# Second product of two feed-forward blocks by a seven-product scheme in two of its three parts, with a weight difference in PSUM and a bias table in another block

## The chip, the core and the metric

The kernel runs on one core of one Trainium2 chip. The metric is device time in microseconds (us), the median of three runs. The engines are called as in the profile: PE (TensorE matmul), PEld (its weight load), DVE (VectorE), ACT (ScalarE), POOL (GpSimd) and SP, which issues most of the DMAs. All data are float32. A matmul whose accuracy matters is made of three: both factors are cut into a high part H (rounded to the type `fp32r`) and a low part L (the rest), and the kernel adds up WH·XH, WH·XL and WL·XH.

## The reference

One step of a two-layer decoder on 512 prompt tokens and 64 sample tokens, which the kernel treats as one matrix of T = 576 columns. The change concerns the feed-forward blocks, of which there are two in each layer (four in all), with D_MODEL = 1024 and D_FF = 2816:

```
def swiglu(x, wi, wo):
    gate, up = jnp.split(x @ wi, 2, axis=-1)
    return (jax.nn.silu(gate) * up) @ wo

for i in range(DEPTH):                     # DEPTH = 2
    h = h + 0.5 * swiglu(rms_norm(h, w['norm_w'][i, 0]), w['ffn1_wi'][i], w['ffn1_wo'][i])
    h = h + mixer(rms_norm(h, w['norm_w'][i, 1]))      # layer 0: RWKV-7; layer 1: windowed attention
    h = h + 0.5 * swiglu(rms_norm(h, w['norm_w'][i, 2]), w['ffn2_wi'][i], w['ffn2_wo'][i])
    h = h + jax.nn.sigmoid(rms_norm(h, w['norm_w'][i, 3]) @ w['pe_gate'][i]) * (p[i] @ w['pe_proj'][i])
```

The attention of layer 1 adds to its logits a bias that depends on the distance alone: three tables, made once from `rel_bias` by a product with a one-hot matrix.

## The kernel before

Everything lies transposed: features on the 128 partitions, the 576 tokens on the free axis, in two halves of HF = 288 columns. So h is eight tiles of 128x576, and the hidden vector of a block has FT = 22 tiles. `ffn` (L368) runs one block. For each hidden tile j a **unit** makes the gate tile, the up tile and u = silu(gate)·up. Units 0 to 4 are plain (`pair`, L375). From unit F_STD = 5 on a unit is `pair7` (L396): gate and up tile, the two halves of the eight k-tiles and the two column halves make a 2x2 by 2x2 block product, which a Strassen-Winograd scheme does in seven block products instead of eight. Each is 4 k-tiles x 3 = 12 matmuls of 128x288, so a unit has 84.

The seven left factors are sums of weight blocks, made in `seven` (L324) for each unit: four loads of 128x512 (`wr`, `sr`), then three sums s1, s2, s4 on DVE into PSUM (L348), one difference s3 = w11 - w21 on POOL into SBUF (L359, tile `ss`), and seven splits (`form`, L337): ACT copies H (L340), and L = a - H (L343) comes from DVE for the three sums in PSUM and from POOL for the other four. The right factors are made once for each block (`forms`, L286). The sums of a unit in PSUM go out through ACT copies to `ev` (L410) and DVE additions (L416, L452); POOL makes the second half of u (L453), and u is split (L159 on ACT, L160 on POOL) into `hv`.

The second product, hidden times `wo`, is plain. It is done in parts, `F_PARTS = (0, 7, 14, FT)`: when the units of a part and one more are through, `wo_part` (L457) takes for each of the eight output tiles n the part's 7 or 8 k-tiles, 3 matmuls each, for both halves; weights are loaded and split by `load_w` (L163: ACT L174, POOL L175), and DVE adds each half to h (L463). The last part has no unit behind it to run ahead. While it runs, `feed` (L217) prepares the next stage as each h tile is done: squares on ACT, their sum on DVE (L273, tile `ssum`), and, where the next stage wants them, the scaled tile's H on ACT (L266) and L on DVE (L267).

`run` calls the blocks in phases with SBUF and PSUM pools of their own: f0 (first block of layer 0), r (RWKV), f1 (second block of layer 0, the gated input `ple`, K and V, first block of layer 1), at (attention) and f2 (second block of layer 1, `ple`). The bias tables are made in f0, by three insertions behind units 9, 12 and 16 (`bias_table`, L1326). In f0 the last part also loads and splits four tiles for `ple` (`ple_load`, L486).

A scheduler sets the order on each engine from the dependencies and the buffers. So weights of a unit are formed while the unit before it runs; `after` (L153) holds some steps behind others. PSUM has eight banks: here four `ps_e`, two `ps_q` and two `ps_d` (`pg`).

Of the kernel before, what the change touches and what calls it, by code (L numbers as in the profile page):

```python
# [16 lines left out]
D = 1024  # L17
DT = D // 128
# [35 lines left out]
N_S7 = 4  # L54
F_PARTS = (0, 7, 14, FT)
# [34 lines left out]
class Body:  # L90
# [124 lines left out]


    def feed(self, *gains, spill=False, start=False, early=(1, S_AT)):  # L217
# [15 lines left out]
        def f(k, half=None):  # L233

            h = self.h[k]
            if half is not None:
                sl = slice(half * HF, (half + 1) * HF)
                sq = self.s(*sv[1]) if k else ssum
# [24 lines left out]
            sq = self.s(*sv[1]) if k else ssum  # L263
# [22 lines left out]
    def forms(self, gain):  # L286
# [7 lines left out]
        def sums(k):  # L294
# [3 lines left out]
            c, e, d = self.bank("q", HF), self.bank("q", HF), self.s("u", 2)[:, h0]  # L298
# [25 lines left out]
    def seven(self, w0, w1, prev):  # L324

        nc = self.nc
        n = DT // 2 * 128
        raw, out = {}, {}
        for i, (nm, w, k) in enumerate((("11", w0, 0), ("21", w1, 0), ("22", w1, n), ("12", w0, n))):
# [4 lines left out]
            nc.sync.dma_start(r, w[:, k:k + n])  # L334
            raw[nm] = r

        def form(i, a, eng):  # L337
# [3 lines left out]
            if not i and prev:  # L341
                self.after(c, prev[1])
            eng.tensor_tensor(L, a, H.bitcast(F32), op=ALU.subtract)  # L343
            out[i] = [(H[:, k * 128:(k + 1) * 128], L[:, k * 128:(k + 1) * 128]) for k in range(DT // 2)]
# [13 lines left out]
        s3 = self.ph.tile([128, n], F32, name="ss", tag="ss", bufs=1)  # L358
        i = nc.gpsimd.tensor_tensor(s3, raw["11"], raw["21"], op=ALU.subtract).ins  # L359
        if prev and prev[2]:  # L360
            self.after(i, prev[2])
        form(4, s3, nc.gpsimd)
# [5 lines left out]
    def ffn(self, wi, wo, done, pre=None, mid=None, fast=None, side=None):  # L368
# [4 lines left out]
        self.n_hv, self.n_t1 = N_HF, 4  # L373

        def pair(j):  # L375
            t1 = self.s("t1", self.n_t1)
            u = self.s("u", 2)
# [15 lines left out]
            hist[j] = self.last_u, hist[j][0], None  # L393
            hv[j] = self.split(u, self.s("hv", self.n_hv, F32R), self.s("hv", self.n_hv, F32R))

        def pair7(j, X):  # L396
            h0, h1 = slice(0, HF), slice(HF, T)
            W = self.seven(wi[j], wi[FT + j], hist[j - 2])
            t1, u = self.s("t1", self.n_t1), self.s("u", 2)
# [54 lines left out]
            hv[j] = self.split(u, self.s("hv", self.n_hv, F32R), self.s("hv", self.n_hv, F32R), nc.gpsimd)  # L454
            hist[j] = i, silu, self.last_l
# [14 lines left out]
        ends = F_PARTS if fast else (0, FH, FT)  # L470
        steps, X = self.forms(fast) if fast else ((), None)
        j = 0
        for a, b in zip(ends, ends[1:]):
# [10 lines left out]
            wo_part(list(range(a, b)), b == FT)  # L484

    def ple_load(self):  # L486
        nc = self.nc
        px = []
        for i in range(2):
            for k in range(PD // 128):  # L490
                p = self.s("u", 2)
# [16 lines left out]
    def ple(self, i, done, tail=False):  # L508
# [760 lines left out]
    def shared_kv(self):  # L1269
# [17 lines left out]
        for n, t in enumerate(ts):  # L1287
# [38 lines left out]
    def bias_table(self, g):  # L1326
# [12 lines left out]
        tr = self.sm("tr", [16, SKW])  # L1339
        nc.vector.tensor_copy(tr, tb[:, TBW - 1 - SKW:TBW - 1][:, ::-1])  # L1340
        nc.scalar.dma_start(self.rev[g * 16:(g + 1) * 16], tr)
# [358 lines left out]
    def run(self):  # L1700
        nc, I = self.nc, self.I
        self.st_tag = (("ssum", 1), ("sq", 2))
        with self.phase("f0", d="e", e=4, q=2, st="q"):
# [11 lines left out]
            self.bias_load()  # L1715
            self.ffn(I["f1wi"][0], I["f1wo"][0], lambda: self.feed(spill=True), pre, self.bias_table, fast="n00", side=self.ple_load)
# [138 lines left out]
```

## Time and profile before

| | us |
|---|---|
| three runs | 2852.56, 2854.98 (median), 2858.19 |
| the profiled execution | 2856.38 |
| its span, first to last instruction | 2854.6 |
| PE busy | 2723.1 (95%) |
| PEld busy | 2540.6 (89%) |
| DVE busy | 1556.9 (55%) |
| POOL busy | 1518.1 (53%) |
| ACT busy | 1298.3 (45%) |

PE is the busy one; the others are busy half of the time on average, which says little of a single stage. So the stages are read one by one: f0's block lies at about 60 to 427 us, the two blocks of f1 at 1110 to 1490 and 1600 to 1990, and that of f2 at 2390 to 2787.

### The profile page before, as it was taken

How to read it: one execution, taken by the hardware profiler on the slowest of the kernel's cores; microseconds unless marked ns; L12 is line 12 of the kernel's file. 1: busy time of each engine (PE TensorE's matmuls, PEld its weight loads, DVE VectorE, ACT ScalarE, POOL GpSimd, SP SyncE). 2: the span in 40 equal slices, each digit the busy share in tenths (PEclk: the TensorE clock that was granted, in tenths of full speed). 3: DMA queues.
4: the chain of work that ended last, by engine and by line, in shares of the span. 5: the costliest groups of instructions: out<-in, count | busy, mean ns of one | idle time of the engine just before them, and what ended most of it. 6: DMA issues, size and time to landing. Idle time of an engine off the chain costs nothing. (4 is left out here: it accounts for less than half of the span.)

```text
span 2854.6 us, 56186 instructions
## 1 busy us (share of the span) xinstructions
PE 2723.1 (95%) x21952; PEld 2540.6 (89%) x21952; DVE 1556.9 (55%) x3300; ACT 1298.3 (45%) x2568; POOL 1518.1 (53%) x1254
## 2 busy tenths in 40 slices
PE   8999997988999999999999999999899999999997
PEld 8999997976767778999999999999888879999997
DVE  6543538457577756633436554243577776533435
ACT  4443535444333225434445444354556655443544
POOL 5665747544243335756654466674544325766753
PEclk9999998999999999999999999999999999999999
DMA  4232234222112112232333223324434443222222
GB/s 137 79 96 85 85 113 139 71 62 55 53 44 75 40 45 80 84 91 85 96 98 103 95 80 95 89 82 120 113 86 104 132 150 115 79 92 86 93 86 96
DMA packets 177085, 257.80 MB, mean 90 GB/s; under 512 B 46889, under 2 KB 70897, under 8 KB 176820
## 3 DMA queue, kind: packets, MB, share of 16 engines
q1 hardware_dynamic: 149312, 224.74, 25.9%
q10 hardware_dynamic: 27508, 29.48, 3.9%
q8 instruction: 172, 2.82, 0.4%
q14 instruction: 93, 0.76, 0.1%
HBM read 234.31 MB, written 19.85 MB: 89 GB/s over the span
## 5 line engine op out<-in xcount | busy, mean ns | idle before, releaser
L175 POOL TENSOR_TENSOR wl<-wr,wh 128x512 fp32r<-128x512 f32 (+2 forms) x477 | 603.3, 1274 | 722.4 <-ACT wh L174 679.9
L201 PE MATMUL ps_e<-hv,wh 128*128 128x288 f32 x2944 | 587.3, 295 | 2.5 <-POOL hv L160 1.3
L174 ACT CAST wh<-wr 128x512 fp32r<-128x512 f32 (+2 forms) x477 | 277.4, 587 | 539.2 <-PE ps_e L201 293.2
L201 PEld LDWEIGHTS ps_e<-hv,wh 128*128 128x128 f32 x2944 | 472.2, 188 | 3.9 <-POOL hv L160 2.2
L201 PE MATMUL ps_e<-hv,wl 128*128 128x288 f32 x1472 | 434.1, 295 | 1.2 <-POOL wl L175 1.2
L558 PE MATMUL ps_d<-x,wh 128*128 128x288 f32 x1664 | 367.6, 308 | 9.1 <-ACT wh L174 3.2
L201 PE MATMUL ps_e<-x,wh 128*128 128x288 f32 x1792 | 364.8, 299 | 11.2 <-ACT x L266 6.9
L201 PEld LDWEIGHTS ps_e<-x,wh 128*128 128x128 f32 x1792 | 291.6, 190 | 13.1 <-ACT x L266 6.9
L558 PEld LDWEIGHTS ps_d<-x,wh 128*128 128x128 f32 x1664 | 273.5, 191 | 29.7 <-issue 9.3
L201 PEld LDWEIGHTS ps_e<-hv,wl 128*128 128x128 f32 x1472 | 276.3, 188 | 1.5 <-POOL wl L175 1.4
L463 DVE SCALAR_TENSOR_TENSOR h<-ps_e,h 128x288 f32<-128x288 f32 x192 | 87.6, 457 | 328.0 <-PE ps_e L201 327.9
L201 PE MATMUL ps_e<-x,wl 128*128 128x288 f32 x896 | 265.6, 297 | 0.0
L558 PE MATMUL ps_d<-x,wl 128*128 128x288 f32 x832 | 249.9, 301 | 0.3 <-POOL wl L175 0.3
L406 PE MATMUL ps_e<-x,wh 128*128 128x288 f32 x1056 | 214.4, 296 | 0.0
L343 POOL TENSOR_TENSOR wl<-wr,wh 128x512 fp32r<-128x512 f32 x136 | 197.0, 1452 | 18.6 <-ACT wh L340 12.7
L406 PEld LDWEIGHTS ps_e<-x,wh 128*128 128x128 f32 x1056 | 170.3, 189 | 3.9 <-issue 3.9
L406 PE MATMUL ps_e<-TH,wh 128*128 128x288 f32 x544 | 162.1, 298 | 9.7 <-DVE t L380 6.9
L201 PEld LDWEIGHTS ps_e<-x,wl 128*128 128x128 f32 x896 | 169.9, 190 | 0.1
L558 PEld LDWEIGHTS ps_d<-x,wl 128*128 128x128 f32 x832 | 158.7, 191 | 2.2 <-issue 0.5
L406 PE MATMUL ps_e<-TH,wl 128*128 128x288 f32 x544 | 160.4, 295 | 0.0
L406 PE MATMUL ps_e<-TL,wh 128*128 128x288 f32 x544 | 159.9, 294 | 0.0
L406 PE MATMUL ps_e<-x,wl 128*128 128x288 f32 x528 | 155.7, 296 | 0.0
(413 smaller groups left out, 6390.3 us busy)
## 6 DMA issues: line engine op xcount, KB each, us to landing
wr<-in_f1wi SPq DMA_DIRECT2D x108, 256.0 KB
wr<-in_f2wi SPq DMA_DIRECT2D x108, 256.0 KB
sr<-in_f1wi SPq DMA_DIRECT2D x68, 256.0 KB
sr<-in_f2wi SPq DMA_DIRECT2D x68, 256.0 KB
wr<-in_f1wo SPq DMA_DIRECT2D x64, 256.0 KB
wr<-in_f2wo SPq DMA_DIRECT2D x64, 256.0 KB
wr<-in_wrkv SPq DMA_DIRECT2D x48, 256.0 KB
wr<-in_wq SPq DMA_DIRECT2D x48, 256.0 KB
```

Source lines behind the costliest of these rows:

```text
L174: nc.scalar.copy(H, raw)
L175: nc.gpsimd.tensor_tensor(L, raw, H.bitcast(F32), op=ALU.subtract)
L201: nc.tensor.matmul(ps[0:nw], a, b[:, sl], start=k + m == 0, stop=3 * k + m == n - 1)
L343: eng.tensor_tensor(L, a, H.bitcast(F32), op=ALU.subtract)
L406: nc.tensor.matmul(ps, a, b, start=first and k + m == 0, stop=k == DT // 2 - 1 and m == 2, skip_group_check=True)
L463: nc.vector.scalar_tensor_tensor(h[:, sl], ps, 0.5, h[:, sl], op0=ALU.mult, op1=ALU.add)
L558: self.nc.tensor.matmul(out, lhsT, rhs, **kw)
```

## The change

In the blocks of f0 and f2 (`deep`) the parts become (0, 6, 14, 22). The first stays plain; the second and the third, 8 hidden tiles each, do the product with `wo` by the same seven-product scheme: two output tiles by two hidden tiles by two column halves, 4 pairs of hidden tiles in a part (`wo_part7`). The left factors come from `seven`, now called with four blocks of `wo`, each a load of four separate runs of 128 columns per partition. The right factors are made from the u tiles of two units (`pair_forms`). All `seven` calls, in all four blocks, make s3 on DVE into a `ps_d` bank and its L on DVE. The tables of the bias move from f0 to the first block of f1, their reversed copy in two halves. `ssum` and `sq` share the buffers of other tiles, and there are three `u` buffers instead of two.

```diff
+N_U = 3
+N_EV = 5
+N_HD = 28
+D_PARTS = (0, 6, 14, FT)
@@ seven
-        s3 = self.ph.tile([128, n], F32, name="ss", tag="ss", bufs=1)
-        i = nc.gpsimd.tensor_tensor(s3, raw["11"], raw["21"], op=ALU.subtract).ins
-        form(4, s3, nc.gpsimd)
+        s3 = self.pg.tile([128, 512], F32, name="ps_d", tag="d")[:, 0:n]
+        nc.vector.tensor_tensor(s3, raw["11"], raw["21"], op=ALU.subtract)
+        form(4, s3, nc.vector)
@@
+    def pair_forms(self, a, b, quick):
+        c, d = self.s("t1", self.n_t1), self.ph.tile([128, HF], F32, name="ev", tag="ev", bufs=N_EV)
+        nc.vector.tensor_tensor(c[:, h0], a[:, h1], a[:, h0], op=sub)
+        nc.vector.tensor_tensor(c[:, h1], b[:, h1], a[:, h1], op=sub)
+        nc.vector.tensor_tensor(d, b[:, h1], c[:, h0], op=sub)
+        nc.vector.tensor_tensor(a[:, h1], b[:, h0], d, op=sub)
+        for i, x in enumerate((c, a, b)):
+            out.append(self.split(x, ..., nc.vector if quick and i < 2 else nc.gpsimd))
+        self.split(d, D[:, 0], D[:, 1], nc.gpsimd)
@@ pair7
-            hv[j] = self.split(u, ..., nc.gpsimd)
+            if j < first7:
+                hv[j] = self.split(u, ..., nc.gpsimd)
+            elif (j - first7) % 2 == 0:
+                pairs[j] = u
+            else:
+                pairs[j - 1] = self.pair_forms(pairs[j - 1], u, j == FT - 1)
@@
+        def wo_part7(js, last):
+            X = [pairs[j] for j in js[0::2]]
+            for n in range(0, DT, 2):
+                W = self.seven(...)
+                if last and not n:
+                    steps = ((C, 1, 0), (A, 0, 4), (B, 3, 5))
+                    for ps, i, x in steps:
+                        prod(ps, i, x, True, range(len(X) - 1))
+                    for ps, i, x in steps:
+                        prod(ps, i, x, False, (len(X) - 1,))
+                    to_h(C, 1, h1)
+                    to_h(A, 0, h0)
+                    to_h(B, 0, h0)
+                    prod(C, 5, 6, False)
+                    to_h(C, 0, h1)
+                    prod(A, 2, 2, False)
+                    to_h(A, 0, h1)
+                    prod(A, 4, 1, False)
+                    to_h(A, 1, h1)
+                else:
...
+                prod(A, 6, 3, False)
+                to_h(A, 1, h0)
+                if f:
+                    f(n)
+                    f(n + 1)
@@ bias_table
-        tr = self.sm("tr", [16, SKW])
+        for c in (0, SKW // 2):
+            tr = self.sm("tr", [16, SKW // 2])
@@ run
-            self.bias_load()
-            self.ffn(I["f1wi"][0], ..., self.bias_table, fast="n00", side=self.ple_load)
+            self.ffn(I["f1wi"][0], ..., fast="n00", side=self.ple_load, deep=True)
+                self.bias_load()
+                self.ffn(I["f2wi"][0], ..., self.pre, self.bias_table, fast="n02")
-            self.ffn(I["f2wi"][1], ..., self.pre, fast="n12")
+            self.ffn(I["f2wi"][1], ..., self.pre, fast="n12", deep=True)
```

`to_h` is the old addition to h (DVE, L525 of the changed kernel, L463 of the old one), seven of them for two output tiles, each behind one of the seven products.

The order moves on DVE in two places. The first is a pair of seven-product units, unit 11 of f0's block before and unit 21 after (`t`, `u` and `ev` are the unit's own tiles, L448 is the old L416; `ps_q`, `sl`, `wl` are weight sums and low parts for the next unit). Before:

```order
L348 TENSOR_TENSOR ps_q<-sr,wr 128x512
L343 TENSOR_TENSOR sl<-ps_q,sh 128x512
L348 TENSOR_TENSOR ps_q<-ps_q,wr 128x512
L343 TENSOR_TENSOR wl<-ps_q,wh 128x512
L348 TENSOR_TENSOR ps_q<-sr,ps_q 128x512
L416 TENSOR_TENSOR t_2365<-ps_d,ev 128x288
L343 TENSOR_TENSOR sl<-ps_q,sh 128x512
L416 TENSOR_TENSOR ev<-ps_e,ev 128x288
L416 TENSOR_TENSOR t_2365<-ps_e,ev 128x288
L452 TENSOR_TENSOR u<-ps_e,t_2365 128x288
```

After, from s3 (L369) on:

```order
L369 TENSOR_TENSOR ps_d<-wr,sr 128x512
L353 TENSOR_TENSOR wl<-ps_q,wh 128x512
L358 TENSOR_TENSOR ps_q<-sr,ps_q 128x512
L448 TENSOR_TENSOR t_4433<-ps_d,ev 128x288
L382 TENSOR_TENSOR t_4535<-u 128x288
L353 TENSOR_TENSOR sl<-ps_q,sh 128x512
L448 TENSOR_TENSOR ev<-ps_e,ev 128x288
L353 TENSOR_TENSOR wl<-ps_d,wh 128x512
L448 TENSOR_TENSOR t_4433<-ps_e,ev 128x288
L383 TENSOR_TENSOR t_4535<-u 128x288
L484 TENSOR_TENSOR u<-ps_e,t_4433 128x288
L384 TENSOR_TENSOR ev<-u,t_4535 128x288
```

Two weight steps (L369 and the L of `ps_d`) and three of the four pair steps (L382 to L384) now stand between the unit's own.

The second place is the start of the last part in f0 (`h_85` are the first two tiles of h, `x_...` the four tiles of `ple_load`). Before:

```order
L416 TENSOR_TENSOR t_4359<-ps_e,ev 128x288
L452 TENSOR_TENSOR u<-ps_e,t_4359 128x288
L463 SCALAR_TENSOR_TENSOR h_85<-ps_e,h_85 128x288
L160 TENSOR_TENSOR x_4603<-u,x_4603 128x576
L160 TENSOR_TENSOR x_4608<-u,x_4608 128x576
L463 SCALAR_TENSOR_TENSOR h_85<-ps_e,h_85 128x288
L160 TENSOR_TENSOR x_4613<-u,x_4613 128x576
L463 SCALAR_TENSOR_TENSOR h_85<-ps_e,h_85 128x288
```

After:

```order
L385 TENSOR_TENSOR u<-u,ev 128x288
L164 TENSOR_TENSOR hv<-t_4535,hv 128x576
L353 TENSOR_TENSOR sl<-ps_q,sh 128x512
L164 TENSOR_TENSOR hv<-u,hv 128x576
L525 SCALAR_TENSOR_TENSOR h_85<-ps_e,h_85 128x288
L164 TENSOR_TENSOR x_4704<-u,x_4704 128x576
L525 SCALAR_TENSOR_TENSOR h_85<-ps_e,h_85 128x288
L358 TENSOR_TENSOR ps_q<-ps_q,wr 128x512
L525 SCALAR_TENSOR_TENSOR h_85<-ps_d,h_85 128x288
L525 SCALAR_TENSOR_TENSOR h_85<-ps_e,h_85 128x288
L369 TENSOR_TENSOR ps_d<-wr,sr 128x512
L164 TENSOR_TENSOR x_4709<-u,x_4709 128x576
```

Behind the last unit there now stand on DVE two splits of pair tiles (L164 `hv`), weight steps, and the four `x` splits between the additions to h, on which the next product into the same bank waits.

## Rows read from the trace of the kernel before

**Rows 1.** The page, part 1: busy us, share of the span, instructions.

```profile
PE 2723.1 (95%) x21952; PEld 2540.6 (89%) x21952; DVE 1556.9 (55%) x3300; ACT 1298.3 (45%) x2568; POOL 1518.1 (53%) x1254
```

**Rows 2.** Windows of 50 us in the blocks: PE, PEld, DVE, ACT, POOL; clock, DMA.

```profile
300.00:350.00 50.00, 50.00 (x364) 47.72 (x363) 26.78 (x48) 26.05 (x51) 36.28 (x29) 1.00 0.27 86
...
2550.00:2600.00 50.00, 50.00 (x380) 50.00 (x380) 25.07 (x46) 27.20 (x53) 39.16 (x32) 1.00 0.32 100
2600.00:2650.00 50.00, 50.00 (x380) 50.00 (x379) 10.14 (x21) 14.24 (x26) 26.68 (x24) 1.00 0.28 81
```

**Rows 3.** Waits of PE, 110 to 400 us: us in total, times, longest.

```profile
PE ps_e L201 <- POOL hv L160: 0.3, 1, 0.3
```

**Rows 4.** Steps of `seven` by line: count, duration in ns, min/median/max.

```profile
L348 DVE TENSOR_TENSOR ps_q<-sr,wr x68: 681/691/1791, 77.3 to 2711.7; 128x512 f32<-128x512 f32 x68
L348 DVE TENSOR_TENSOR ps_q<-ps_q,wr x68: 677/690/692, 80.3 to 2713.7; 128x512 f32<-128x512 f32 x68
...
L343 POOL TENSOR_TENSOR wl<-wr,wh x136: 1277/1305/1810, 76.9 to 2723.0; 128x512 fp32r<-128x512 f32 x136
...
L343 DVE TENSOR_TENSOR wl<-ps_q,wh x68: 691/692/694, 81.9 to 2716.6; 128x512 fp32r<-128x512 f32 x68
...
L359 POOL TENSOR_TENSOR ss<-wr,sr x68: 1278/1292/1308, 66.7 to 2714.9; 128x512 f32<-128x512 f32 x68
```

**Rows 5.** Other DVE steps by line, the same columns.

```profile
L463 DVE SCALAR_TENSOR_TENSOR h<-ps_e,h x192: 444/458/459, 124.7 to 2785.0; 128x288 f32<-128x288 f32 x192
...
L302 DVE TENSOR_TENSOR hv<-hv,u x16: 442/444/448, 39.0 to 2443.7; 128x288 f32<-128x288 f32 x16
...
L160 DVE TENSOR_TENSOR hv<-u,hv x20: 757/1319/1846, 33.7 to 2458.6; 128x576 fp32r<-128x576 f32 x20
...
L267 DVE SCALAR_TENSOR_TENSOR x<-h,vecs,x x54: 505/836/1834, 6.9 to 2786.5; 128x576 fp32r<-128x576 f32 x42, 128x288 fp32r<-128x288 f32 x12
...
L273 DVE TENSOR_TENSOR ssum<-ssum,sq x53: 444/746/1845, 12.2 to 2828.8; 128x576 f32<-128x576 f32 x41, 128x288 f32<-128x288 f32 x12
```

**Rows 6.** Timeline, two DVE steps back to back: start, duration in us.

```profile
284.05 0.69 DVE L343 TENSOR_TENSOR sl<-ps_q,sh 128x512 fp32r<-128x512 f32 x1 [0.65 <-ACT sh L340]
284.66 0.69 DVE L348 TENSOR_TENSOR ps_q<-ps_q,wr 128x512 f32<-128x512 f32 x1
```

**Rows 7.** Timeline around the last unit's end in f0 (its last matmul ends at about 375.6).

```profile
374.66 0.69 ACT L148 ACTIVATE t<-t 128x576 f32<-128x576 f32 x1 [1.62 <-DVE t L416]
375.37 1.28 ACT L144 ACT_TABLE_LOAD   x1
376.66 0.67 ACT L159 CAST hv<-u 128x576 fp32r<-128x576 f32 x1
...
375.80 0.46 DVE L452 TENSOR_TENSOR u<-ps_e,t 128x288 f32<-128x288 f32 x1 [1.17 <-PE ps_e L406]
...
375.43 0.80 POOL L453 TENSOR_TENSOR u<-ev,t 128x288 f32<-128x288 f32 x1 [1.01 <-ACT t L148]
377.41 1.43 POOL L160 TENSOR_TENSOR hv<-u,hv 128x576 fp32r<-128x576 f32 x1 [1.19 <-ACT hv L159]
...
378.90 0.40 PE L201 MATMUL ps_e<-hv,wh 128*128 128x288 f32 x1 [0.30 <-POOL hv L160]
```

**Rows 8.** Timeline, DVE behind the last matmul of f0's block.

```profile
427.19 0.46 DVE L463 SCALAR_TENSOR_TENSOR h<-ps_e,h 128x288 f32<-128x288 f32 x1 [1.68 <-PE ps_e L201]
428.54 0.46 DVE L273 TENSOR_TENSOR ssum<-ssum,sq 128x288 f32<-128x288 f32 x1 [0.89 <-ACT sq L271]
```

**Rows 9.** DMA queue q1, at 250 to 300 us: packets, MB, share of 16 engines.

```profile
q1 hardware_dynamic: 2666, 4.54, 30.7%
```

**Rows 10.** The same at 442.5 to 443.5 us.

```profile
q1 hardware_dynamic: 214, 0.14, 51.5%
```

More of the change, by code (lines that the diff above doesn't have):

```diff
@@ L322, in forms, with seven @@
         return [lambda k=k: sums(k) for k in range(DT // 2)] + [quarters], out
-    def seven(self, w0, w1, prev):
+    def seven(self, blocks):
         nc = self.nc
-        n = DT // 2 * 128
+        n = 512
+        prev = self.units[-2] if len(self.units) > 1 else None
         raw, out = {}, {}
-        for i, (nm, w, k) in enumerate((("11", w0, 0), ("21", w1, 0), ("22", w1, n), ("12", w0, n))):
+        for i, nm in enumerate(("11", "21", "22", "12")):
             if i % 2:
@@ L340, in form @@
             c = nc.scalar.copy(H, a).ins
-            if not i and prev:
+            if not i and prev and prev[1]:
                 self.after(c, prev[1])
             eng.tensor_tensor(L, a, H.bitcast(F32), op=ALU.subtract)
-            out[i] = [(H[:, k * 128:(k + 1) * 128], L[:, k * 128:(k + 1) * 128]) for k in range(DT // 2)]
+            out[i] = [(H[:, k * 128:(k + 1) * 128], L[:, k * 128:(k + 1) * 128]) for k in range(4)]
         def diff(a, b, op):
@@ L372, in ffn @@
         hv, hist = {}, {}
-        self.n_hv, self.n_t1 = N_HF, 4
+        self.units = []
+        self.n_hv, self.n_t1 = N_HD if deep else N_HF, 4
+        ends = D_PARTS if deep else F_PARTS if fast else (0, FH, FT)
+        first7 = ends[1] if deep else FT
+        pairs = {}
         def pair(j):
             t1 = self.s("t1", self.n_t1)
-            u = self.s("u", 2)
+            u = self.s("u", N_U)
             def ev_g(half, ps, sl):
@@ L397, in pair7 @@
             h0, h1 = slice(0, HF), slice(HF, T)
[L398 to L399 removed]
+            n = DT // 2 * 128
+            W = self.seven({f"{a + 1}{b + 1}": wi[a * FT + j][:, b * n:(b + 1) * n] for a in range(2) for b in range(2)})
+            t1, u = self.s("t1", self.n_t1), self.s("u", N_U)
             A, C, B = self.bank("e", HF), self.bank("e", HF), self.pg.tile([128, HF], F32, name="ps_d", tag="d")
@@ L483, in ffn @@
                 j += 1
-            wo_part(list(range(a, b)), b == FT)
+            (wo_part7 if deep and a else wo_part)(list(range(a, b)), b == FT)
     def ple_load(self):
@@ L1714, in run @@
                 f(k)
-            self.bias_load()
-            self.ffn(I["f1wi"][0], I["f1wo"][0], lambda: self.feed(spill=True), pre, self.bias_table, fast="n00", side=self.ple_load)
+            self.ffn(I["f1wi"][0], I["f1wo"][0], lambda: self.feed(spill=True), pre, fast="n00", side=self.ple_load, deep=True)
         with self.phase("r", d=0, st="d", i=2, x=1, y=1, q=1, w=1):
```

87 lines of the change are left out of this document (64 added, 23 removed).

## The prediction, made before the changed kernel was run

> **What bounds the kernel now.** I read the page's busy times first: PE is busy 95% of the span and no other engine over 55% [rows 1]. An average hides stages, so next come the windows inside the feed-forward blocks. In a stretch of units and in a stretch of the old second product alike PE is busy for all of 50 us and runs 380 matmuls of 128x288 (2550 to 2650 us, [rows 2]), at the full clock (1.00, the 2.4 GHz level). 50 / 380 = 0.1316 us is what one matmul costs there; the 295 ns that the profile gives for one is a pipelined duration and no price. Third, the waits: from 110 to 400 us PE waits once, for 0.3 us [rows 3]. So inside these blocks the count of matmuls is the time, and DVE and POOL, at half and three quarters of the stretch with units (25.1 and 39.2 of 50 us), are hidden. A matmul taken away there is worth 0.1316 us until another engine becomes late.
>
> **What is taken away.** A part of 8 hidden tiles took 8 output tiles x 8 k-tiles x 2 halves x 3 = 384 matmuls. By sevens it takes 4 output pairs x 7 products x 4 pairs x 3 = 336. Two such parts in two blocks: 4 x 48 = 192 matmuls fewer. The first part's change from 7 to 6 tiles only moves work. 192 x 0.1316 = **-25.3 us**, all of it on the path.
>
> **What it costs on DVE in the units.** Before, a unit gives DVE three sums and three L's of 512 columns and four steps of 288: 6 x 0.69 + 4 x 0.46 = 6.0 us [rows 4, 5] in a unit of 84 x 0.1316 = 11.05 us. The move of s3 and its L adds 2 x 0.69 = 1.4 us, in all four blocks; in the two deep ones every second unit also gets four subtractions of 288, 4 x 0.44 = 1.8 us (priced by L302, which also has two inputs in SBUF). That is 9.1 of 11.05 us: covered, if nothing blocks. POOL loses s3 (1.29) and an L (1.3) per unit and gains, per pair of units, splits of 576 and 288 (1.43 + 0.8 us) [rows 4, 7], so it gets lighter. ACT gains 0.67 + 0.4 us per pair, on some 6 of 11 us.
>
> What may show is order, not load. The step c[h1] (L383) waits for POOL's u[h1], which in rows 7 is ready about 0.6 us after the unit's end, and the last evacuation of the unit (L484) stands behind it, then ACT's split of a behind that. ACT frees the bank for the next unit's third product with a copy queued behind two such splits. Adding up these steps I get that copy some 0.2 us before PE wants the bank. So each of the 14 pairs that has units behind it costs PE between nothing and 0.4 us: 0 to 6 us, and I take **+2**, nearer to nothing because the sum says just in time.
>
> **The second product in the middle parts.** A unit of it lasts 11.05 us as well and gives DVE eight steps of 512 and seven of 288: 8 x 0.69 + 7 x 0.46 = 8.7 us; each addition has at least one product (1.58 us) of slack before its bank is wanted. Covered: 0.
>
> **The start of the last part** is where the cover is gone: nothing runs ahead there. Before, u of the last unit was ready 0.66 us after the end, ACT's copy came at 1.1 (behind a table load), POOL's L at 1.9 to 3.3 us, and PE, with 21 matmuls to do without it, stood for 0.3 us [rows 7]. Now 27 matmuls (3.55 us) stand ahead, but the chain is longer. Counting from the unit's end, with a step behind another starting 0.08 us before its end [rows 6]: c[h1] 0.7 to 1.1, u 1.5, d 1.8, s1 of the next weights 2.5, a[h1] 2.9; DVE's split of c (1.3 us, L160 in [rows 5]) 4.1, a weight step 4.7, split of a 6.0. PE wants a at 4.1: a stand of 1.9 us. Then DVE has a backlog, and each product into bank A waits for the addition to h ahead of it. In f0 the four splits of `ple_load`, 1.3 us each, stand between these additions: the products wait twice more, 1.65 and 1.35 us by the same count. With the first 0.1 more (an ACT copy in between) that is 5.0 us, less the 0.3 of before: **+4.7**. In f2 there are no such splits, but each of the four units also carries `feed`: 2 x (0.84 + 0.75) = 3.2 us [rows 5], so that DVE has 11.9 us to do in 11.05. Counted through: 3.2 us in the first unit, 0.55 and 1.0 in the last two, less 0.3: **+4.4**. If the splits run at their shortest (0.76), f0 keeps 2 to 3 us and f2 as much; if every one takes 1.8, both come to 7 to 8.
>
> **The end of f0's block.** Before, DVE's last addition starts at 427.19 and the last sum of squares ends at 429.0 [rows 8]. Now the last two tiles are prepared together, and a sum of 576 stands between them: 0.75 us later, on the chain to RWKV's start: **+0.7**. In f2 the gate product has enough matmuls without these tiles.
>
> **The bias tables** cost PE some 16 matmul places per insertion (364 in place of 380 per 50 us, one insertion in that window [rows 2]), in f0 now and in f1 then: 0, with 2 us either way because s3 now shares its banks with the tables. At the kernel's start two small loads fall away from the DMA queues: 0 to -1, I take **-0.5**.
>
> **The loads of `wo`** come in runs of 512 bytes, four times the packets. Now a packet of 1.7 KB costs 0.307 x 16 x 50 / 2666 = 92 ns [rows 9], and in a stretch of short ones (0.65 KB) 0.515 x 16 / 214 = 38.5 ns [rows 10]. A unit's 2048 packets then take 2048 x 38.5 / 16 = 4.9 us of 11.05: hidden. At 92 ns it would be 11.8 us and the loads would bound 16 units: +12 us at most. The short row is far nearer: 0.
>
> **Sum**: -25.3 + 2 + 4.7 + 4.4 + 0.7 - 0.5 = -14.0. The profiled execution took 2856.4 us (span 2854.6), 1.4 above the median of the runs; against the median, 2855.0 - 14 = **2841 us**.
>
> **Rivals.**
>
> (A) Nearly the full gain: DVE runs its splits at the shortest, since POOL is lighter, and the walk above overstates. Stands of 3 to 5 us in all: 2855 - 25.3 + 4 = 2834 us. For it: the median s1 takes 691 ns beside a POOL that is busy 78% of the time. Against: half of the splits in rows 5 take over 1.3 us.
>
> (B) Hiccups in each pair: the copies on ACT come a little late in all 14 pairs (0.6 to 0.8 us), or the loads do; 10 us more, 2851 us. That is within 0.2%, about what a measurement of this kernel can tell from no change. For it: the count above leaves 0.2 us. Against: a pair's first unit has 3 us of spare DVE time.
>
> (C) Slower: DVE and POOL shut each other out. The same step with both inputs in SBUF takes 681 to 1791 ns, with one in PSUM never over 692 [rows 4]; the split of two SBUF tiles takes 757 to 1846 ns on DVE [rows 5]. So a DVE step with two SBUF inputs sometimes waits up to a POOL step (1.3 us). The change puts six such steps more into each pair of units (two s3, four subtractions). If each lost 1.3 us, DVE would have 6.0 x 2 + 2.8 + 1.8 + 7.8 = 24.4 us for 22.1: PE late by 2.3 us in 14 pairs, 32 us, and the last parts later too: 2855 - 14 + 32 = 2873 us. It decides against the change from about 1 us lost per step: the spare time of a pair, 22.1 - 16.6 = 5.5 us, plus 14 / 14 pairs, over six steps. Against: half of the s1 take 691 ns, so most are not blocked.
>
> The Trainium skill has this as a rule ("SBUF — State Buffer", section "Who interferes with whom"): a DVE instruction with two SBUF inputs contends with a GpSimd instruction that reads SBUF, and whichever issues second fully blocks until the first is done. The trace agrees on the spread (691 to 1791 ns); taken at its worst for every such step the rule gives rival C, taken as often as s1 shows it, nothing.
>
> (D) That the change doesn't do what it says: only if PE's matmuls did not fall by 192. The program's order has 192 fewer, so I give this no chance of its own.
>
> **Chances.** My forecast, a gain of 6 to 20 us: 0.62. A: 0.18. B and the loads: 0.11. C: 0.09. The likeliest is the forecast: 2841. The range takes in most of A and reaches to B: 2831 to 2850. Faster by over 0.2% (5.7 us): 0.62 + 0.18 = 0.80; within 0.2%: 0.11; slower: 0.09.
>
> **What will show it.** Right: 192 matmuls fewer; windows of 50 us inside the deep parts still with 380 matmuls; PE waits of some 5 us for DVE (L525, L164) in the first unit of the last part of f0 and f2, and DVE full there. The pair term: PE waits in `ps_e` for ACT's `ev` copies, once per pair. C would show as s3 and L382 to L385 with durations above 1 us in most of their runs. The bias would show as a difference in f1 alone. The forecast is wrong if PE stands inside the units by more than 0.5 us per pair, or if the stands at the last parts differ from 3 to 8 us each.

## The result, and the profile after

The changed kernel takes 2893.01 us (median of 4 runs, 2892.58 to 2899.7), the kernel before 2856.36 us (median of 4, 2852.56 to 2858.19): a ratio of 1.0136, 95% interval 1.0117 to 1.0154. It is slower by 1.4%, where I forecast 2841 us and gave "slower" a chance of 0.09. The profiled execution has a span of 2890.9 us, 36.3 more than before.

The page's first part, as in [rows 1]: PE has its 192 matmuls fewer and is no longer busy for as large a share; DVE has 291 us more, POOL 123 us less.

```profile
PE 2724.6 (94%) x21760; PEld 2539.6 (88%) x21760; DVE 1848.0 (64%) x3683; ACT 1329.0 (46%) x2648; POOL 1395.2 (48%) x1130
```

Windows of 50 us as in [rows 2] (after the stretch: PE, PEld, DVE, ACT, POOL with their counts; clock, DMA share, GB/s). The second line lies in the middle part's second product, the others in units:

```profile
150.00:200.00 50.00, 44.55 (x322) 44.10 (x322) 37.23 (x53) 24.73 (x49) 30.28 (x24) 0.97 0.27 85
250.00:300.00 50.00, 50.00 (x379) 50.00 (x379) 37.07 (x67) 19.96 (x35) 22.69 (x16) 1.00 0.32 96
300.00:350.00 50.00, 44.51 (x311) 44.05 (x310) 36.87 (x53) 24.15 (x47) 29.44 (x23) 0.93 0.25 80
2550.00:2600.00 50.00, 44.44 (x321) 43.98 (x320) 36.97 (x52) 25.48 (x50) 31.23 (x23) 0.96 0.22 71
```

The new second product is as forecast, 379 matmuls in 50 us. The units are not: PE stands for 5.5 of 50 us, and even in its busy time it does fewer matmuls than 44.5 / 0.1316 = 338. DVE, at 37 of 50 us, is not full. The waits of PE (us in total, times, longest) in f0's block, 100 to 440 us, where [rows 3] had one of 0.3 us:

```profile
PE ps_e L438 <- ACT ev L442: 19.2, 7, 2.8
PE ps_e L521 <- DVE hv L164: 2.5, 2, 1.6
```

f2 has the same 19.2 us in 7 stands: one stand of 2.75 us for each of the 14 pairs that has units behind it, and in each PE waits for a copy on ACT. Four DVE steps with both inputs in SBUF (s1, s3, and d and a[h1] of the pair step; ns min/median/max), as in [rows 4]:

```profile
L358 DVE TENSOR_TENSOR ps_q<-sr,wr x84: 683/692/1926, 78.6 to 2800.0; 128x512 f32<-128x512 f32 x84
L369 DVE TENSOR_TENSOR ps_d<-wr,sr x84: 677/1216/1697, 67.8 to 2800.6; 128x512 f32<-128x512 f32 x84
L384 DVE TENSOR_TENSOR ev<-u,t x16: 448/1189/1197, 159.2 to 2768.1; 128x288 f32<-128x288 f32 x16
L385 DVE TENSOR_TENSOR u<-u,ev x16: 450/1542/1546, 162.1 to 2769.1; 128x288 f32<-128x288 f32 x16
```

The median of s1 is what it was, but d and a[h1] are at 1.19 and 1.54 us in the median, with 0.45 as the shortest. The timeline shows one pair (start, duration in us, in brackets the idle time ahead and what ended it). First DVE and POOL from the end of the pair's second unit on:

```profile
158.45 0.46 DVE L383 TENSOR_TENSOR t<-u 128x288 f32<-128x288 f32 x1 [1.65 <-POOL u L485]
158.83 0.45 DVE L484 TENSOR_TENSOR u<-ps_e,t 128x288 f32<-128x288 f32 x1
159.19 1.18 DVE L384 TENSOR_TENSOR ev<-u,t 128x288 f32<-128x288 f32 x1
160.30 1.92 DVE L358 TENSOR_TENSOR ps_q<-sr,wr 128x512 f32<-128x512 f32 x1
162.13 1.54 DVE L385 TENSOR_TENSOR u<-u,ev 128x288 f32<-128x288 f32 x1
...
158.56 1.51 POOL L353 TENSOR_TENSOR wl<-wr,wh 128x512 fp32r<-128x512 f32 x1
160.03 1.64 POOL L164 TENSOR_TENSOR hv<-t,hv 128x576 fp32r<-128x576 f32 x1
161.62 1.75 POOL L353 TENSOR_TENSOR wl<-wr,wh 128x512 fp32r<-128x512 f32 x1
```

DVE's d ends 0.30 us behind POOL's first step, s1 0.55 us behind the second, a[h1] 0.30 us behind the third: each is issued while a POOL step runs, and is through only when that step is. Then ACT and PE (the next unit's three copies out of PSUM, L442, are called `p1`, `e5` and `u2` in the code: those of its first, second and third product):

```profile
160.04 0.39 ACT L442 COPY ev<-ps_e 128x288 f32<-128x288 f32 x1
163.72 0.67 ACT L163 CAST hv<-u 128x576 fp32r<-128x576 f32 x1 [3.28 <-DVE u L385]
164.29 0.58 ACT L350 CAST sh<-ps_q 128x512 fp32r<-128x512 f32 x1
164.77 0.67 ACT L163 CAST hv<-u 128x576 fp32r<-128x576 f32 x1
165.34 0.40 ACT L442 COPY ev<-ps_e 128x288 f32<-128x288 f32 x1
165.63 0.44 ACT L163 CAST hv<-ev 128x288 fp32r<-128x288 f32 x1
165.97 0.63 ACT L350 CAST sh<-sr 128x512 fp32r<-128x512 f32 x1
166.49 0.41 ACT L442 COPY ev<-ps_e 128x288 f32<-128x288 f32 x1
...
166.94 0.40 PE L438 MATMUL ps_e<-TH,wh 128*128 128x288 f32 x1 [2.67 <-ACT ev L442]
```

ACT stands 3.28 us for a[h1] and has the copies `e5` and `u2` queued behind it; PE wants `u2`'s bank for the unit's fifth product. That is the whole stand. The lower clock shows in short windows around another stand, the one at 312 to 316 us (columns as above, for PE, PEld, DVE, ACT, POOL):

```profile
312.00:314.00 2.00, 0.86 (x7) 0.63 (x5) 0.78 (x2) 1.66 (x4) 0.91 (x1) 1.00 0.00 0
314.00:316.00 2.00, 0.43 (x3) 0.44 (x4) 2.00 (x3) 2.00 (x6) 2.00 (x3) 1.00 0.00 0
316.00:318.00 2.00, 2.00 (x11) 2.00 (x10) 1.97 (x4) 0.00 (x1) 2.00 (x2) 0.52 0.14 34
318.00:320.00 2.00, 2.00 (x12) 2.00 (x12) 1.56 (x3) 1.07 (x2) 0.30 (x1) 0.62 0.79 260
320.00:322.00 2.00, 2.00 (x18) 2.00 (x17) 0.55 (x2) 0.69 (x1) 0.16 (x1) 1.00 0.30 112
```

PE comes back from the stand at about half the granted clock (the 1.2 GHz level) for some 3 us, doing 11 and 12 matmuls in 2 us in place of 15 or more. Not every stand has this: behind the one at 164 us the windows stay at 1.00. In the trace's record of the granted clock, 11 of the 14 pair stands are followed by such a stretch.

**Where the 36 us are.** I cut the one profiled execution of each kernel into four stretches: f0's block (first matmul of a unit by sevens to the start of the last addition to h), f2's block, what lies between, and the rest (not in the table). "Ideal" is e1_nodeep below, which has no second product by sevens, less 96 x 0.1316 = 12.6 us per block.

| kernel | f0 | between | f2 |
|---|---|---|---|
| before | 343.5 | 2024.7 | 333.1 |
| after | 351.1 | 2026.7 | 357.4 |
| e1_nodeep | 331.3 | 2034.4 | 331.4 |
| "ideal" | 318.7 | | 318.8 |
| e3_latesplit | 329.7 | 2028.8 | 332.1 |
| e4_late | 326.8 | 2024.9 | 329.7 |
| e5_onepsum | 321.2 | 2025.0 | 325.4 |
| e6_poolzero | 317.4 | 2035.4 | 317.9 |
| e7_s3pool | 343.5 | 2030.4 | 345.7 |
| e8_late2 | 323.3 | 2030.1 | 327.3 |
| e9_psumpair | 324.8 | 2025.3 | 329.3 |
| e12_psumtwo | 327.7 | 2035.6 | 334.3 |

Over the ideal the changed kernel has 32.4 us in f0 and 38.6 in f2. Of these 19.2 each are the pair stands, 2.5 and 4.2 the last parts' (the waits in `ps_e` of L521), and the rest, 10.7 and 15.2, is nearly all the clock: in f0's four windows of units PE's busy time had room for 88 matmuls more than it did (88 x 0.1316 = 11.6 us), in f2's six from 2500 us on for 108 (14.2 us). The record of the clock agrees: its stretches at 0.5 cost 10.2 us in f0 and 15.3 in f2. Of these 25.5 us some 19 come right behind pair stands, the others behind PE's waits in the last parts and at the start of f2's units.

### The profile page after: what moved, and what is told of

Same layout as the page of the kernel before. It is cut to its first block, busy times and chain, and to the rows that moved or that the text cites. A ratio compares the mean times of both kernels' runs of the same rounds, so it can differ in the third digit from the quotient of the medians.

```text
span 2890.9 us, 55999 instructions
## 1 busy us (share of the span) xinstructions
PE 2724.6 (94%) x21760; PEld 2539.6 (88%) x21760; DVE 1848.0 (64%) x3683; ACT 1329.0 (46%) x2648; POOL 1395.2 (48%) x1130
## 4 chain that ended last, share of the span: by engine, by line
PE 75%; DVE 14%; ACT 4%; issue 3%; POOL 2%; DMA 1%; ACTq 0%; DVEq 0%; SPq 0%; POOLq 0%
PE ps_e L205 22%; PE ps_e L438 20%; PE ps_d L649 11%; PE ps_e L521 5%; PE ps_d L438 3%; PE ps_i L649 2%; PE ps_s L649 2%; PE ps_q L649 2%; PE ps_w L649 2%; PE ps_x L649 1%; DVE ps_q L358 1%; PE ps_o L649 1%; PE ps_pt L658 1%; ACT sh L350 1%; DVE S L1448 1%
## 5 line engine op out<-in xcount | busy, mean ns | idle before, releaser
L179 POOL TENSOR_TENSOR wl<-wr,wh 128x512 fp32r<-128x512 f32 (+2 forms) x413 | 521.2, 1272 | 651.7 <-ACT wh L178 617.6
L178 ACT CAST wh<-wr 128x512 fp32r<-128x512 f32 (+2 forms) x413 | 237.6, 582 | 434.7 <-PE ps_e L205 217.1
L205 PE MATMUL ps_e<-hv,wh 128*128 128x288 f32 x1920 | 383.4, 295 | 1.9 <-ACT wh L178 1.3
L353 POOL TENSOR_TENSOR wl<-wr,wh 128x512 fp32r<-128x512 f32 x168 | 260.5, 1553 | 150.4 <-ACT wh L350 144.7
L205 PEld LDWEIGHTS ps_e<-hv,wh 128*128 128x128 f32 x1920 | 308.2, 188 | 2.7 <-ACT wh L178 1.5
L205 PEld LDWEIGHTS ps_e<-x,wh 128*128 128x128 f32 x1792 | 290.6, 189 | 12.6 <-ACT x L274 7.2
L205 PE MATMUL ps_e<-hv,wl 128*128 128x288 f32 x960 | 283.1, 295 | 1.2 <-POOL wl L179 1.2
L205 PE MATMUL ps_e<-x,wl 128*128 128x288 f32 x896 | 265.0, 297 | 0.0
L205 PEld LDWEIGHTS ps_e<-hv,wl 128*128 128x128 f32 x960 | 180.7, 188 | 1.5 <-POOL wl L179 1.4
L485 POOL TENSOR_TENSOR u<-ev,t 128x288 f32<-128x288 f32 x68 | 55.3, 814 | 258.7 <-ACT t L152 241.4
L350 ACT CAST sh<-ps_q 128x512 fp32r<-128x512 f32 x168 | 98.3, 585 | 160.6 <-DVE ps_q L358 151.8
```

The costliest lines, as they stand in the source:

```text
L178: nc.scalar.copy(H, raw)
L179: nc.gpsimd.tensor_tensor(L, raw, H.bitcast(F32), op=ALU.subtract)
L205: nc.tensor.matmul(ps[0:nw], a, b[:, sl], start=k + m == 0, stop=3 * k + m == n - 1)
L350: c = nc.scalar.copy(H, a).ins
L485: nc.gpsimd.tensor_tensor(u[:, h1], c22, t1[:, h1], op=ALU.mult)
```

## The experiments

The theory (T) from this reading: DVE steps that need SBUF twice are held for as long as a POOL step runs, d, s1 and a[h1] one after the other; ACT's queue, in order, hands the delay to PE. Its rivals: R1, the order on ACT alone (four splits ahead of the copies) makes the stands, however long DVE takes; R2, the third weight sum and its low part, moved to DVE, make it late; R3, the loads of `wo` or the last parts; R4, the bias table in the middle block. All ratios are to the kernel before, run beside them on the same chip (median 2852.1 to 2853.5 us there). The edits are shortened: `...` stands for what is left out, and the comments in them are mine.

**e1: the changed kernel without its second product by sevens.**

```diff
-            self.ffn(I["f1wi"][0], ..., side=self.ple_load, deep=True)
+            self.ffn(I["f1wi"][0], ..., side=self.ple_load)
-            self.ffn(I["f2wi"][1], ..., fast="n12", deep=True)
+            self.ffn(I["f2wi"][1], ..., fast="n12")
```

> Second product by sevens left out (21952 matmuls again), the sum s3 in PSUM and on DVE and the bias table in the middle block kept. Theory T (the loss is made in the pair steps of the two deep blocks: DVE and POOL shut each other out there, ACT's queue passes it to PE): no stand of 2.7 us in ps_e for ACT's ev copies, s3 covered, 2852 to 2861 us. Rival R2 (the third sum and its L on DVE make DVE late in every unit): stands remain in the units, at least +10 us over before, 2866 us or more. Rival R4 (the bias table costs more in the middle block than it did in the first): a time above before with all of the difference between 1050 and 1500 us.

2852.15 us, ratio 0.9994 (0.9981 to 1.0006). No pair stands. The time is that of the kernel before, so the bias table costs much the same in either place, and R4 falls. In blocks: with the tables f0 took 10.4 us more than f2 before (343.5 against 333.1), and without them takes 331.3; f1's first block, cut in the same way, went from 333.1 to 341.8 us, while its second is at 332.3. (The whole stretch between is 9.7 us longer, but it varies by as much from one kernel to the next where the code is the same, so that is no measure.) s3 alone does nothing (R2 falls for units without pair steps). Everything that is lost comes with the second product by sevens. Of R3 little is left: the second product ran 379 matmuls in 50 us with its `wo` loads, and the last parts' waits are 6.7 us.

**e2: one SBUF tile for d and a[h1].**

```diff
-        nc.vector.tensor_tensor(d, b[:, h1], c[:, h0], op=sub)
-        nc.vector.tensor_tensor(a[:, h1], b[:, h0], d, op=sub)
+        nc.vector.tensor_scalar(d, b[:, h1], self.vec("n00", 0), None, op0=ALU.mult)
+        nc.vector.tensor_scalar(a[:, h1], d, self.vec("n00", 0), None, op0=ALU.mult)
```

> As the changed kernel, but the pair steps d and a[h1] (L384, L385) read one SBUF tile each, not two: d is a scaled b[h1], a[h1] a scaled d (the subtracted parts are left out); same queue, same place, same readers. T: the two steps fall from 1.19 and 1.54 us to about 0.45 each, ACT's split of a comes some 1.8 us earlier, and the stand per pair falls from 2.75 us to under 1 us; with 14 pairs and the lower clock behind the stands 2845 to 2868 us. Rival R1 (ACT's order alone does it, however long these steps take): stands of over 2 us remain, 2885 to 2895 us. Rival R2 (s1 and s3 are what is blocked): stands fall by less than 0.8 us, 2875 to 2890 us.

2887.16 us, 1.0114 (1.0091 to 1.0137), stands of 2.4 us. But the edit did not do what I wanted: the steps stayed long (the like step of the first product's forms, L310, was changed by the same edit; it took 0.36 us there).

```profile
L385 DVE TENSOR_SCALAR u<-ev,vecs x16: 363/1393/1400, 160.1 to 2763.7; 128x288 f32<-128x288 f32 x16
```

Read alone, this would have spoken for R1. It only says that "two SBUF inputs" was too narrow a name for what is held; e5 and e11 take that up.

**e3 and e4: the order moved.** In e3 the four splits of a pair stand on ACT behind the next unit's copy u2; in e4 the whole pair step is written behind the next unit's addition of C:

```diff
                 u2 = copy(A)
+                while todo:      # e3: splits of the pair before, each held behind u2 on ACT
+                    q, f = todo.pop()
+                    pairs[q] = self.pair_splits(*f, False, self.last_copy)
...
                 add(C, u2, t1[:, h1])
+                while todo:      # e4: the whole pair step here instead
+                    q, x, y = todo.pop()
+                    pairs[q] = self.pair_forms(x, y, False)
```

> As the changed kernel, but the four splits of each pair that is not a block's last stand on ACT behind the next unit's third copy (u2); the four subtractions stay where they are on DVE. T: d and a[h1] still take 1.2 and 1.5 us, since POOL still works beside them (less, as its own split of c moves too), but nobody waits: the 14 stands of 2.75 us and the clock drops behind them go, 2833 to 2848 us. Rival R3 (the loads of wo in short runs, or the last parts, make the loss): the stands stay or turn up in other waits, 2870 us or more. Rival R2 (DVE is too full with s3 and the four steps): PE waits for DVE's additions instead, 2860 us or more.

> As e3_latesplit, but the whole of the pair step, subtractions too, is moved behind the next unit's addition of C. T: the subtractions meet POOL's own weight steps there, so they are still stretched, over 0.8 us in the mean; ACT's split of a now stands ahead of the unit after's first copy, for which PE has 3 products (8 us) of slack: no stands, 2833 to 2850 us. If stands of over 1 us remain, now in the wait for the first copy p1 or for the silu, the place of the step matters more than T says: 2855 us or more.

e3: 2851.76 us, 0.9989 (0.9973 to 1.0005). The stands fall from 2.75 to 0.87 us each, and the clock stays at 1.00 in the windows of units: the whole loss is gone, but also the whole gain, 4 us over my range of 2833 to 2848. The wait and DVE's d in it:

```profile
PE ps_e L446 <- ACT ev L450: 6.1, 7, 0.9
...
L386 DVE TENSOR_TENSOR ev<-u,t x16: 448/1182/1194, 158.2 to 2725.1; 128x288 f32<-128x288 f32 x16
```

d and s1 are still held, and ACT's H of s1 and s2, ahead of `u2` as ever, now carries what is left of the delay. a[h1], which I had expected at 1.5 us, is not held any more (0.45 us in the median): POOL's split of c has moved away from it. e4: 2841.39 us, 0.9963 (0.9946 to 0.9980), faster than before and in my range. No stand per pair, although a[h1] still takes 0.93 us (0.45 unheld): nobody waits for it there. d is not held in its new place (0.45 us), against my expectation. Two waits for POOL's last split, 2.8 us together, appear at the start of each middle part. So ACT's order is one link of the chain, as T and R1 both have it; but as both edits also changed what POOL does beside the pair steps, they can't tell T from R1.

**e5 and e6: the order kept, the hold removed.** In e5 d and a[h1] read PSUM for their second input; in e6 POOL only writes in the deep blocks.

```diff
-        nc.vector.tensor_tensor(d, b[:, h1], c[:, h0], op=sub)
-        nc.vector.tensor_tensor(a[:, h1], b[:, h0], d, op=sub)
+        nc.vector.tensor_tensor(d, b[:, h1], ps, op=sub)      # e5: ps is the unit's bank A
+        nc.vector.tensor_tensor(a[:, h1], d, ps, op=sub)
...
-            eng.tensor_tensor(L, a, H.bitcast(F32), op=ALU.subtract)
+            nc.gpsimd.memset(L.bitcast(F32), 0.0)             # e6, where eng is POOL
```

> As the changed kernel, but the pair steps d and a[h1] read their second input from PSUM (the unit's own bank A) in place of the SBUF tile; what they should subtract is left out. Same queue, place and readers, all four splits still ahead of u2 on ACT. e2_oneside had left the steps stretched (1.04 and 1.39 us) with a scaled copy from SBUF to SBUF, so it tested nothing. T, in the form that a DVE step is held by POOL when it needs more than its one SBUF read: both steps fall to about 0.45 us, a is ready 1.8 us earlier, the stand per pair falls from 2.75 us to 0.5 to 1.3 us (s1 is still held), 2850 to 2868 us. Rival R1 (ACT's order alone, whatever DVE takes): over 2 us per pair, 2885 to 2895 us. If the steps stay over 1 us, POOL isn't what holds them by their inputs.

> As the changed kernel, but in the two deep blocks POOL only writes zeros where it computed the low parts of weights and of the pair forms (its subtractions are left out; u[h1] stays); DVE's and ACT's work is the same, ACT's splits still stand ahead of u2. T: with POOL reading nothing there, s1, s3, d and a[h1] all take their shortest, 0.69 and 0.45 us; stands per pair 0 to 0.5 us, 2833 to 2850 us. R1: stands of over 2 us stay, 2885 us or more. R2 (DVE too full by count of its steps): stands of 1 us or more in waits for DVE.

e5: 2834.77 us, 0.9944 (0.9926 to 0.9962). The two steps are at their shortest in all 16 runs, the stands are gone altogether, and the units run 380 matmuls per 50 us at a clock of 1.00. All four splits still stand ahead of `u2` (the scheduler put the copy `e5` ahead of one of them, no more), and 14 of the 16 d, as of the 16 a[h1], lie wholly inside a POOL step that reads SBUF. R1 falls.

```profile
L384 DVE TENSOR_TENSOR ev<-u,ps_e x16: 444/446/447, 159.0 to 2706.0; 128x288 f32<-128x288 f32 x16
L385 DVE TENSOR_TENSOR u<-ev,ps_e x16: 439/442/451, 160.3 to 2707.0; 128x288 f32<-128x288 f32 x16
...
150.00:200.00 50.00, 50.00 (x380) 50.00 (x379) 37.56 (x63) 28.93 (x58) 33.93 (x26) 1.00 0.31 104
2550.00:2600.00 50.00, 50.00 (x380) 50.00 (x379) 39.32 (x68) 26.93 (x52) 35.77 (x26) 1.00 0.33 99
```

It did better than the 0.5 to 1.3 us per pair that I expected (2850 to 2868 us), partly since s1 was held for less, too (1.07 us in a pair that I looked at). e6: 2824.83 us, 0.9905 (0.9890 to 0.9920), with no stands in units and hardly any in the last parts; that is 8 us under my range. d and a[h1] have their two SBUF tiles again, and yet take 0.45 us in all runs; s3's median is back at 0.69. a[h1] lies wholly inside a zeroing on POOL in 14 of 16 runs, the first of them in the last two lines (start, duration in us):

```profile
L387 DVE TENSOR_TENSOR ev<-u,t x16: 447/449/452, 155.1 to 2708.1; 128x288 f32<-128x288 f32 x16
L388 DVE TENSOR_TENSOR u<-u,ev x16: 450/452/455, 156.0 to 2709.0; 128x288 f32<-128x288 f32 x16
L372 DVE TENSOR_TENSOR ps_d<-wr,sr x84: 678/692/1693, 66.0 to 2734.5; 128x512 f32<-128x512 f32 x84
...
156.04 0.45 DVE L388 TENSOR_TENSOR u<-u,ev 128x288 f32<-128x288 f32 x1
...
155.96 1.10 POOL L396 MEMSET hv<- 128x576 f32 x2
```

So it takes both: a DVE step that goes to SBUF twice, and a POOL step that reads SBUF. POOL was also faster in e6 (a zeroing of 128x512 takes 0.53 us, not 1.3), so how much of its last 10 us under e5 is the hold's is not shown.

The Trainium skill ("SBUF — State Buffer", section "Who interferes with whom") has the same condition: a DVE instruction with two SBUF inputs contends with a GpSimd instruction that reads SBUF, not with one that only writes. The runs agree on both halves, 1.19 and 1.54 us beside reading steps, 0.45 beside writing ones.

**e7: s3 back on POOL in the deep blocks.**

```diff
-        s3 = self.pg.tile([128, 512], F32, name="ps_d", tag="d")[:, 0:n]
-        nc.vector.tensor_tensor(s3, raw["11"], raw["21"], op=ALU.subtract)
-        form(4, s3, nc.vector)
+        s3 = self.ph.tile([128, n], F32, name="ss", tag="ss", bufs=1)      # where deep
+        nc.gpsimd.tensor_tensor(s3, raw["11"], raw["21"], op=ALU.subtract)
+        form(4, s3, nc.gpsimd)
...
```

> As the changed kernel, but in the two deep blocks the third weight sum and its low part are back on POOL, in an SBUF tile. T: the pair steps meet a POOL that is busier; d and a[h1] still 1.2 to 1.5 us, stands of 2 to 4 us per pair, 2885 to 2910 us. R2 (the move of s3 to DVE is the cause): the stands go, 2835 to 2855 us.

2876.09 us, 1.0089 (1.0074 to 1.0104): between the two ranges. Now c[h1] and a[h1] are the ones held (1.53 and 1.67 us in the median), d is not, and PE stands twice per pair, about 0.85 and 1.15 us, 28.5 us in all where the changed kernel has 38.4. So the hold comes with the pair steps wherever s3 is. R2's move is worth some 13 us of the loss (36.7 us over the kernel before, run beside it, against 23.6 here). The move shifts which steps meet, and the stands are single and longer with it, with the low clock behind them; here PE's windows of units stay at 1.00.

**e8: e4 with the middle part begun like the last.**

```diff
-                if last and not n:
+                if not n:
```

> As e4_late, which had 2841 us and two waits of 1.4 us for POOL's last split at the start of each middle part; now the first pair of output tiles of the middle part also begins with its three products over the first three pairs of u, as the last part does: 27 matmuls (3.6 us) ahead of the last pair's forms. T: the waits for POOL there go (2 x 2.8 us) and nothing takes their place, 2833 to 2838 us. If the waits for the splits are not what costs there: 2839 to 2843 us.

2838.58 us, 0.9958 (0.9943 to 0.9973). The waits for POOL at the middle parts shrink from 2.8 to 1.0 us each; the time is 2.8 us under e4's, but the intervals overlap, and it lies just above the range of T (2833 to 2838). It has the lowest median of the kernels that compute everything; e4, e9 and e10 can't be told from it.

**e9, e10 and e12: e5's cure with the whole computation.** c[h0] and d go into the unit's own banks C and A, whose sums have been read by then.

```diff
-    def pair_forms(self, a, b, quick):
+    def pair_forms(self, a, b, quick, c0, d):      # banks C and A of the unit
...
+        nc.vector.tensor_tensor(c0, a[:, h1], a[:, h0], op=sub)
+        nc.vector.tensor_tensor(c1, b[:, h1], a[:, h1], op=sub)
+        nc.vector.tensor_tensor(d, b[:, h1], c0, op=sub)
+        nc.vector.tensor_tensor(a[:, h1], b[:, h0], d, op=sub)
...
```

e9 splits each of the seven forms by itself, e10 adds e8's edit, e12 keeps the four splits and computes c[h0] twice (SBUF and PSUM).

> The whole computation. The pair step's c[h0] and d are written into the unit's own two PSUM banks (C and A, whose sums have been read by then), so that d and a[h1] read one SBUF tile and one PSUM tile; each of the seven forms is split by itself, c[h0] and d on DVE, the rest on POOL, so the parts that need only a finished u come early. T: d and a[h1] 0.45 us, no stand per pair, and the stands at the last parts shrink too, since their first three products need only raw halves: the 25.3 us of the matmuls less 2 to 6 us are kept, 2826 to 2834 us beside 2852.5 of before. If ACT's five splits per pair ahead of u2 are what matters (R1), stands of 1 us or more per pair, 2850 us or more.

> As e9_psumpair, with the middle part's first pair of output tiles also begun by its three products over the first three pairs of u (as in e8_late2). If POOL's last splits are still late at the start of the middle part, 1 to 3 us less than e9_psumpair; if not, the same within 1 us.

> The whole computation, as near to e5_onepsum as it can be had: c[h0] is computed twice, once into SBUF for its split and once into the unit's bank C, d is written into bank A, so that d and a[h1] read one SBUF and one PSUM tile; four splits per pair as in the changed kernel, d's low part on DVE. T: no stands per pair (e5_onepsum had none, e9_psumpair with seven splits by form had 14 of 0.35 us), d and a[h1] 0.45 us, 2832 to 2840 us beside some 2853 of before. If the number of ACT's splits is not what made the small stands in e9_psumpair but the place of s1 (held by POOL), they stay at 0.3 us or more, 2840 to 2846 us.

e9: 2843.20 us, 0.9960 (0.9945 to 0.9974). e10: 2843.68 us, 0.9962 (0.9949 to 0.9974), no gain over e9. e12: 2849.17 us, 0.9984 (0.9972 to 0.9996). e9 and e10 beat the kernel before by 0.4%, e12 can hardly be told from it. e9 misses my 2826 to 2834 us and e12 both of its ranges; e10 came out as the second case that I gave it. d and a[h1] are at 0.45 us in each, but small stands remain, 0.35 us per pair in e9 and 0.6 in e12. Here is e12's wait in f0:

```profile
PE ps_e L439 <- ACT ev L443: 3.9, 7, 0.6
```

In e9 these stands (4.8 us) and the last parts' waits (1.8 and 4.7 us) are 11 of the 16.6 us that its two blocks have over the ideal; the rest I did not trace. c[h1], which still reads two SBUF tiles, takes 0.91 us in the median of its 16 runs there (0.46 in the changed kernel). In e12 the scheduler put s1 ahead of d. s1 still reads two SBUF tiles, is held (1.43 us in the pair looked at), and delays a[h1] from in front. In both the hold had moved to another step in the chain. That e12's times in the table are so far above e5's, 10 us of it between the blocks where the code is the same, is in part luck of the profiled executions: 2853.65 us for e12, above its median, and 2828.85 for e5, below.

**e11: plain copies.**

```diff
-        nc.vector.tensor_tensor(d, b[:, h1], c[:, h0], op=sub)
-        nc.vector.tensor_tensor(a[:, h1], b[:, h0], d, op=sub)
+        nc.vector.tensor_copy(d, b[:, h1])
+        nc.vector.tensor_copy(a[:, h1], d)
```

> As the changed kernel, but the pair steps d and a[h1] are plain copies of one SBUF tile into another (d copies b[h1], a[h1] copies d; the subtractions are left out): one SBUF input, no vector operand, unlike e2_oneside. If a DVE step is held by POOL only through a second SBUF input, 0.45 us at most each and a time near e5_onepsum, 2828 to 2845 us. If a copy from SBUF to SBUF is held as well, some of the two steps take over 1 us and stands of 1 to 2.5 us per pair stay, 2865 to 2890 us.

A single run: 2907.05 us beside 2853.5, above my 2865 to 2890, with stands of 3.4 us. The copies are short where they can be (0.30 us) and held like the subtractions otherwise:

```profile
L384 DVE COPY ev<-u x16: 299/1040/1047, 159.2 to 2782.4; 128x288 f32<-128x288 f32 x16
L385 DVE COPY u<-ev x16: 301/1364/1366, 162.0 to 2783.2; 128x288 f32<-128x288 f32 x16
```

The same section of the Trainium skill says that copies and `tensor_scalar` can enter a mode with two ports and then contend as well; e2 and e11 agree with it, and e5 shows the kind of step that does not (one SBUF tile, one PSUM tile).

## Why the prediction was wrong, point by point

- **The matmuls**: right. 192 fewer, and where nothing stands (units of e5 and e6, the second product itself) each is worth 0.1316 us: 379 to 380 in 50 us.
- **The pair term, "+2"**: wrong: 38.4 us of stands, with the clock behind them enough for the whole error of 50 us. The step that failed is the walk along the queues, "Adding up these steps I get that copy some 0.2 us before PE wants the bank", with d and a[h1] priced by L302 at 0.44 us and s1 at its median. The sum before it, "9.1 of 11.05 us: covered, if nothing blocks", was right as a sum; its condition did not hold. None of L302's 16 runs in the kernel before starts inside a POOL step, and the median s1 at most in the last 0.03 us of one; the pair step starts when POOL's u[h1] is done, and POOL's next steps start there too. In the pair above, the three held steps lost 0.73 + 1.23 + 1.09 = 3.05 us. My own count left 0.2 us of slack at the copy `u2`; 3.05 - 0.2 = 2.85 us, against a mean of 2.74 us measured. So the order of the walk was right, and three durations in it were wrong.
- **The clock** had no term. Behind 11 of the 14 stands of 2.7 us comes a stretch at about half clock: some 19 us, half as much again as the stands, and 26 us with those behind PE's other waits. In e3, with stands of 0.87 us, the windows of units stay at 1.00.
- **The last parts, "+4.7" and "+4.4"**: PE waits 2.5 us in f0 and 4.2 us in f2; before it was 0.3 each. In f0 the wait for the splits was near (1.9 us forecast), but the two waits behind the `ple_load` splits, 3 us, did not come: only one of the four splits took 1.5 us, the others 0.75. So f0 is outside the 3 to 8 us that I had named. In f2 the sum was near, less so its places: 2.0 us for the splits and 2.2 for additions, most of that in one wait.
- **The end of f0's block, "+0.7"**: from the last addition's start to the end of the last sum it was 1.8 us [rows 8] and is 2.4: 0.6.
- **Bias, s3 in plain units, `wo` loads, all 0**: right (e1; 379 matmuls per 50 us in the middle part).
- **The sum without the hold** of d and a[h1]: e5 has -17.7 us where I had -14. That is near, but e5's s1 is still held, and two terms of the sum (the clock, f0's last part) were off, so part of it is luck.
- **The -0.5 for the loads at the start** was not tested by any run.
- **Rival C** had the mechanism, and the wrong way for it to act. It charged lost time against DVE's spare time in a pair and decided "from about 1 us lost per step". DVE never ran out (37 of 50 us). What decided was the latency of one chain, with ACT's queue (rival B's place) behind it and the clock on top: 37 us over before in place of C's 18. And its argument against, "half of the s1 take 691 ns, so most are not blocked", used an average over places for steps with a fixed place: 14 of the 16 d and a[h1] are held, the two others, in the last pairs, are not.

## What to carry to other kernels

Price a DVE step that goes to SBUF twice by what POOL does at that very place in the program, not by its median elsewhere; if POOL's next steps are released by the same event, count the rest of a POOL step for each of them (here 0.7 to 1.2 us), and follow the delay through every in-order queue behind it. To get rid of it, give one operand a PSUM bank that is just free, or write the step later, behind the copies that others wait for; check in the trace which step is held next. A stand of some us on PE can cost more than its length (here half as much again), since the clock may come back low.

## What the runs showed that I had not expected

- A DVE copy of 128x288 from SBUF to SBUF, with one input, is held by POOL as a subtraction with two is (0.30 us free, 1.04 and 1.36 us in the median), while a subtraction of an SBUF and a PSUM tile never was (439 to 451 ns in 32 runs).
- POOL steps are stretched as well: a low part of 128x512 (L353) takes 1.27 us at its shortest, 1.60 in the median, and 1.51 and 1.75 us beside the held DVE steps shown above.
- The stretch between the two blocks, with the same code there, took 2024.9 to 2035.6 us in the changed kernels of this study. f1's two blocks took 341.7 to 342.0 and 332.2 to 332.8 us in every one of them, so the spread lies in the other stages. What sets it was not tried; it is of the size of the differences among the last kernels, which is why these are compared by their blocks.
